# The first column pair of an up projection: norm sum, loads and sums of the second token half in another order

## The chip, the core and the metric

One core of a Trainium2 chip. Its engines work side by side, each through its own fixed list of instructions: PE (TensorE, matmuls into PSUM), DVE (VectorE), ACT (ScalarE), POOL (GpSimd) and SP, whose queue issues the DMAs of this kernel. An instruction waits on semaphores of other engines, and what is behind it on its engine waits with it. The metric is the time of one execution on the device in microseconds, as the median of several runs.

## The reference

One layer of a decoder trunk for 1024 prompt tokens and 64 sample tokens, width 1024, in float32. After the recurrent branches the layer ends with a gated convolutional feed-forward block; this is the part that matters here (the rest is left out):

```
x = x + gt1[:, None] * (merged @ p['w_out'])
h = modulate(x, p['g_norm2'], sh2, sc2)          # rmsnorm over the width, then scale and shift
up = h @ p['w_up']                               # 1024 -> 6144
uc, new_ffn_conv = causal_dwconv(ffn_conv, up, p['ffn_conv_w'], p['ffn_conv_b'])
ua, ub = jnp.split(uc, 2, axis=-1)
x = x + gt2[:, None] * ((jax.nn.gelu(ua) * ub) @ p['w_down'])
```

## The kernel before

Channels lie on the 128 partitions, tokens along the free dimension. The tokens are worked on in two halves: A (512 prompt tokens and the 64 sample tokens, 576 columns) and B (the other 512 prompt tokens). A float32 matmul is made of three passes at the rate of a rounded type: each operand is split into a rounded high part (a copy on ACT) and the remainder (a subtraction on DVE), and high x high, high x low and low x high are added up in PSUM (`split_form`, L1156, for tokens; `split_to` in `take`, L1275, for weights: `wh` and `wl` in the profile).

The up projection (`up`, L1455) goes through 24 column blocks of `w_up`, 256 columns each. Each block is a 2 x 2 block product (two column halves, even and odd width blocks, two token halves), done with seven products instead of eight. Of the weights A11, A12, A21, A22 the sums S1 to S4 are made; of the tokens the forms B11 and B21 (half A, even and odd blocks), B22 (half B, odd blocks), T1 = half B even less half A even, T2 = B22 less T1, T3 = B22 less half B even, T4 = half A odd less T2 (signs as in the code). The products are p1 = A11 B11 and p4 = A22 T4 and p6 = S2 T2 (kind "w", 576 columns), p2 = A12 B21 (also "w"), p3 = S4 B22 and p5 = S1 T1 (kind "e", 512 columns), p7 = S3 T3 (kind "p"). p1, p6, p7 and p4 add up in one PSUM tile `b`, and in between what has been reached is copied or added out of it: p4 can add into `b` only once p7's evacuation (L1400) has read it. `finish` (L1471) then does the short convolution, the gelu and the product of the two parts.

The forms are made once and kept. B11 and B21 are made early (`h2a`). The forms with half B need the second norm of half B: the output projection `w_out` (L1112) writes its result `x2d` to memory and sums its squares into `acc2`; the last two squares stay apart (`last`). `rstd_from` (L353) adds these three up over the partitions by matmuls with ones (`prs`), takes the square root on ACT and the reciprocal on DVE (`rB2`, in the profile `rstdB`). `h2b` (L1198) then reads x2d back block by block (`x2B`, three buffers), multiplies it by rB2 on DVE and applies scale and shift on ACT (`norm_raw`, L1194), subtracts half A's forms that it loads from `h2d` (`hA`), and makes B22, T1, T2, T3, T4; of the subtractions those for T3 and T4 run on POOL.

All this falls into `up_lead` (L1410), which does the first column blocks of both parts (0 and 12) together: the products p1 and p2 of both, which need only half A, then the norm sum, the conditioning row `sada` with its transposes `adap` (`ada_tail`, L1443, 16 slow float32 matmuls with `araw` from memory), `h2b`, and then the products with half B. The last p4 of each block is done within the next block.

The order in which instructions stand on each engine is fixed by a scheduler, roughly by the order of the code; `high_priority(offset=n)` lets what it encloses stand as if it had been written n steps earlier. Buffers of a pool are reused in turn, and an instruction that writes one waits for the last reader.

Of the kernel before, what the change touches and what calls it, by code (L numbers as in the profile page):

```python
# [51 lines left out]
def _body(ctx, nc, tc, a):  # L52
    V, S, G, T_ = nc.vector, nc.scalar, nc.gpsimd, nc.tensor
# [41 lines left out]
    def slot(i, name, dt=F32R):  # L95
        return pp.tile([128, 2, 576], dt, tag=f"P{i}", name=name)

    def slot512(i, name, dt=F32):
        return slot(i, name, dt).rearrange("p r x -> p (r x)")[:, :1024].rearrange("p (r x) -> p r x", r=2)
# [46 lines left out]
    def psum(tag, shape, name):  # L146
        return ps.tile(shape, F32, tag=tag, name=name, bufs={"mm": 3, "ms": 2}[tag])

    def mm(name):
        return psum("mm", [128, 2, 512], name)  # L150

    def one(tag, shape, name, dt=F32, bufs=1):
        return (rp if tag.startswith(RIGHT) else ph).tile(shape, dt, tag=tag, name=name, bufs=bufs)

    def tmp(tag, shape, name, dt=F32, bufs=2):
        return (rp if rp is not None and tag in ("xc", "h") else tp).tile(shape, dt, tag=tag, name=name, bufs=bufs)
# [196 lines left out]
    def rstd_from(acc, n, name, tag="rstd", out=None):  # L353
        pr = psum("ms", [128, 512], "prs")[:, :n]
        acc = acc if isinstance(acc, list) else [acc]
        for i, x in enumerate(acc):
            T_.matmul(pr, ones, x, start=i == 0, stop=i == len(acc) - 1)
        return rstd_of(pr, name, tag, out)

    def rstd_of(pr, name, tag="rstd", out=None):  # L360
        n = pr.shape[1]
        sd = rg("sd")[:, :n] if out is None else out[:, :n]
        S.activation(sd, pr, AF.Sqrt, scale=1.0 / D, bias=epst)
        if out is not None:
            r = out[:, :n]
        else:
            r = tmp(tag, [128, 512], name, bufs=1)[:, :n] if n > 64 else tmp("rstds", [128, 64], name, bufs=1)
        V.reciprocal(r, sd)
        return r
# [331 lines left out]
    x2d = [dp.tile([1024, 512], F32, name=f"x2d{h}") for h in range(2)]  # L701
# [445 lines left out]
    def form(n, j):  # L1147
        if n in FORMS:
            x = slot(FORMS[n][j], f"{n}_{j}")
            x = x[:, :, :512] if n == "B22" else x  # L1150
        else:
            x = one(f"{n}_{j}", [128, 2, 512], f"{n}_{j}", F32R)
        F[n, j] = x
        return x

    def split_form(x, f):  # L1156
        S.activation(x[:, 0], f, AF.Copy)  # L1157
        V.tensor_sub(x[:, 1], f, x[:, 0].bitcast(F32))  # L1158
# [8 lines left out]
    def halves(x):  # L1167
        return x.rearrange("p (h c) -> p h c", h=2)
# [25 lines left out]
    def norm_raw(dst, x, rstd, kb):  # L1194
        V.tensor_mul(x, x, rstd)
        S.activation(dst, x, AF.Identity, scale=gmod["g2"][:, kb, 0:1], bias=modT[:, 24 + kb, 0:1])

    def h2b():  # L1198

        A, ST = [], []  # L1200

        def load(tag, k, bufs):
            t = tmp(tag, [128, 632], "hA", bufs=bufs)[:, :576]
            nc.sync.dma_start(t, h2d[k])
            return t

        def nb2(dst, k):
            t = tmp("xc", [128, 632], "x2B", bufs=3)[:, :512]
            nc.sync.dma_start(t, x2d[1][k * 128:(k + 1) * 128])
            norm_raw(dst, t, rB2, k)  # L1210

        for j in range(4):
            ST.append(slot512(4 + j, f"h2B{j}"))
            nb2(ST[j][:, 1], 2 * j + 1)
            split_form(form("B22", j), ST[j][:, 1])
        for j in range(4):
            A.append(load("gl", 2 * j, 4))
        for j in range(4):
            nb2(ST[j][:, 0], 2 * j)
            V.tensor_sub(A[j][:, 32:544], ST[j][:, 0], A[j][:, 32:544])  # L1220
            split_form(form("T1", j), A[j][:, 32:544])
            G.tensor_sub(ST[j][:, 0], ST[j][:, 1], ST[j][:, 0])
        for j in range(4):
            V.tensor_sub(A[j][:, 32:544], ST[j][:, 1], A[j][:, 32:544])
            split_form(form("T2", j), A[j])
        for j in range(4):
            c = load("xc", 2 * j + 1, 3)
            G.tensor_sub(A[j], c, A[j])
        for j in range(4):
            split_form(form("T3", j), ST[j][:, 0])  # L1230
        for j in range(4):
            split_form(form("T4", j), A[j])

    def prod(acc, kind, wt, n, start=False, stop=False):
# [16 lines left out]
    class Blocks:  # L1251
# [5 lines left out]
        def load(self, *names):  # L1257
            for n in names:
                t = self.t.setdefault(n, None)
                if t is None:  # L1260
                    t = self.t[n] = wt("wr", f"w{n}", F32, WR)
                nc.sync.dma_start(t, self.w[{"A11": 0, "A12": 1, "A21": 2, "A22": 3}[n]])
# [18 lines left out]
    def wt(tag, name, dt, bufs):  # L1281
        return uw.tile([128, 512], dt, tag=tag, name=name, bufs=bufs)
# [105 lines left out]
    def evac_up(b, part, gl):  # L1388
        m0 = 24 * part + 2 * b
        raw = {}  # L1390

        def evac(i, half, y, z, e=None):
            t = tmp("rx", [128, 656], "up", bufs=4)
            o = t[:, 32:544] if half else t[:, :576]
            o = halves(o) if len(y.shape) == 3 else o
            with tc.high_priority(offset=400):
                if z is None:
                    S.activation(o, y, AF.Copy)
                elif e is not None:
                    V.tensor_sub(o, y, z)  # L1400
                    V.tensor_add(o, o, e)
                else:
                    V.tensor_add(o, y, z)  # L1403
            raw[i, half] = t
            if (i, 1 - half) in raw:
                finish(i, raw, part, m0 + i, gl, 2 * b + i)

        return evac

    def up_lead():  # L1410

        nonlocal rB2
        gl = {}
        Q = [Quad(q, evac_up(0, i, gl)) for i, q in enumerate(lead)]
        for i in range(2):
            if i == 1:
                x = slot512(2, "wx")
                Q.append(Quad(Blocks(a["w_up"][12], (("A11", x[:, 0]), ("A12", x[:, 1]))), evac_up(0, 1, gl)))
                Q[1].q.load("A11", "A12")
            Q[i].p1()  # L1420
            Q[i].p2()
        rB2 = slot(3, "rstdB2", F32)[:, 0, :512]
        rstd_from(acc2, 512, "rstdB2", out=rB2)
        e = mm("e")
        ada_tail()
        h2b()
        Q[0].p3_first(e[:, 0])
        with tc.high_priority(offset=300):
            Q[1].q.load("A21", "A22")
            Q[1].q.sums(G)  # L1430
        Q[1].p3_first(e[:, 1])
        for q in Q:
            q.p5_last()
        Q[0].p6()
        Q[0].c12()
        Q[0].p7()
        Q[0].p4()
        Q[1].p6()
        Q[1].c12()
        Q[1].p7()  # L1440
        return Q[1]

    def ada_tail():  # L1443
# [11 lines left out]
    def up():  # L1455
        pend = up_lead()
        for b in range(1, 12):
            gl = {}
            for part in range(2):
                q = Quad(blocks_of(a["w_up"][12 * part + b]), evac_up(b, part, gl))  # L1460
                q.p1()
                pend.p4()
                q.p5()
                q.p6()
                q.p2()
                q.p3()
                q.p7()
                pend = q
        pend.p4()

    def finish(i, raw, part, m, gl, k):  # L1471
        for half in range(2):
            t = fix(half, raw[i, half], m)
            n = UN[half]
            if part == 0:
                gl[i, half] = tmp("gl", [128, 632], "gl", bufs=4)
                g = gl[i, half][:, :n]
                conv_up(t, m, g)
                S.activation(g, g, AF.Gelu_apprx_tanh)
                continue  # L1480
            u, g = tmp("xc", [128, 632], "uc", bufs=3), gl[i, half]
            conv_up(t, m, u[:, :n])
            if half == 0:
                c = tmp("cs", [128, 64], "cs", bufs=2)
                G.tensor_mul(two4(s8(c)), useg(u), useg(g))
                nc.sync.dma_start(actd[0][k][:, :64], c)
            V.tensor_mul(u[:, :512], u[:, :512], g[:, :512])
            nc.sync.dma_start(actd[half][k][:, 512 * half - 512:] if half else actd[0][k][:, 64:576], u[:, :512])
# [140 lines left out]
    acc2 = w_out(0, mgA)  # L1629
# [9 lines left out]
    acc2 = w_out(1, mgB)  # L1639
# [10 lines left out]
    rB2 = None  # L1650
# [161 lines left out]
```

## Time and profile before

| | us |
|---|---|
| median of three runs | 1767.33 (1766.81 to 1769.57) |
| profiled execution, its own time | 1769.02 |
| its span, first to last instruction | 1767.2 |
| PE busy | 1707.3 (97%) |
| DVE busy | 1246.5 (71%) |
| ACT busy | 913.9 (52%) |
| POOL busy | 228.6 (13%) |

Granted TensorE clock over the span: 0.988 of full speed. The rows further down are lines of that one profiled execution. In a timeline a row begins with the start from the span's start and the duration; "x4" means four such instructions merged, and a bracket names the idle time before it and what ended it. In names, "b<-B,wh" means tile `b` written from tiles `B` and `wh`, buffer numbers left out.

### The profile page before, as it was taken

How to read it: one execution, taken by the hardware profiler on the slowest of the kernel's cores; microseconds unless marked ns; L12 is line 12 of the kernel's file. 1: busy time of each engine (PE TensorE's matmuls, PEld its weight loads, DVE VectorE, ACT ScalarE, POOL GpSimd, SP SyncE). 2: the span in 40 equal slices, each digit the busy share in tenths (PEclk: the TensorE clock that was granted, in tenths of full speed). 3: DMA queues.
4: the chain of work that ended last, by engine and by line, in shares of the span. 5: the costliest groups of instructions: out<-in, count | busy, mean ns of one | idle time of the engine just before them, and what ended most of it. 6: DMA issues, size and time to landing. Idle time of an engine off the chain costs nothing.

```text
span 1767.2 us, 29386 instructions
## 1 busy us (share of the span) xinstructions
PE 1707.3 (97%) x10542; PEld 1536.3 (87%) x10542; DVE 1246.5 (71%) x2621; ACT 913.9 (52%) x1608; POOL 228.6 (13%) x496
## 2 busy tenths in 40 slices
PE   7999999999999999999988999999999979999997
PEld 3899999899997877888766999999999968999887
DVE  8878688967846787766749877777777755336426
ACT  4557658535535588745436655555454544224224
POOL 0012110100000001020013322222222220000000
PEclk9999999999999999999998999999999989999999
DMA  8276334366646654356653222222222228546634
GB/s 302 78 231 177 99 108 132 121 192 196 204 127 203 214 177 150 118 162 189 208 173 87 74 81 84 75 74 74 74 75 79 80 85 258 166 133 188 197 96 137
DMA packets 151826, 250.87 MB, mean 142 GB/s; under 512 B 34048, under 2 KB 43264, under 8 KB 151680
## 3 DMA queue, kind: packets, MB, share of 16 engines
q1 hardware_dynamic: 151680, 248.99, 45.6%
q8 instruction: 83, 1.36, 0.3%
q14 instruction: 63, 0.52, 0.1%
HBM read 205.20 MB, written 43.73 MB: 141 GB/s over the span
## 4 chain that ended last, share of the span: by engine, by line
PE 68%; DVE 6%; DMA 4%; ACT 2%; issue 1%; SPq 0%; POOL 0%; POOLq 0%; DVEq 0%; ACTq 0%
PE mm L226 15%; PE b L1246 13%; PE mm L224 13%; PE e L1242 7%; PE mm L1533 7%; PE a L1246 4%; PE b L1249 4%; DMA al<-act 2%; DVE wlo L179 1%; DMA xB<-x 1%; PE pg L961 1%; PE pv L787 1%; PE sada L274 1%; PE sada L273 1%; PE sx L717 0%
## 5 line engine op out<-in xcount | busy, mean ns | idle before, releaser
L179 DVE TENSOR_TENSOR wlo<-raw,whi 128x512 fp32r<-128x512 f32 x310 | 214.5, 692 | 207.6 <-ACT whi L178 181.7
L178 ACT ACTIVATE whi<-raw 128x512 fp32r<-128x512 f32 x310 | 194.4, 627 | 316.2 <-PE mm L224 105.2
L224 PE MATMUL mm<-h1A,whi 128*128 128x288 f32 x1024 | 184.3, 299 | 0.0
L226 PE MATMUL mm<-h1B,whi 128*128 128x512 f32 x512 | 159.9, 393 | 0.0
L224 PEld LDWEIGHTS mm<-h1A,whi 128*128 128x128 f32 x1024 | 152.3, 190 | 0.2
L1246 PE MATMUL b<-T,wh 128*128 128x288 f32 x768 | 134.9, 297 | 2.1 <-DVE up L1403 1.3
L1246 PEld LDWEIGHTS b<-T,wh 128*128 128x128 f32 x768 | 115.1, 189 | 5.3 <-issue 1.5
L245 ACT ACTIVATE wh<-wA 128x512 fp32r<-128x512 f32 x94 | 59.2, 630 | 110.3 <-PE b L1246 42.0
L226 PEld LDWEIGHTS mm<-h1B,whi 128*128 128x128 f32 x512 | 95.6, 188 | 23.0
L224 PE MATMUL mm<-h1A,wlo 128*128 128x288 f32 x512 | 111.3, 298 | 2.1 <-DVE wlo L179 2.1
L226 PE MATMUL mm<-h1B,wlo 128*128 128x512 f32 x256 | 100.6, 393 | 0.7 <-DVE wlo L179 0.7
L224 PE MATMUL mm<-act,whi 128*128 128x288 f32 x512 | 91.8, 300 | 2.4 <-ACT act L1157 1.3
L1381 DVE SCALAR_TENSOR_TENSOR uc<-up,vec,uc 128x624 f32<-128x624 f32 (+1 forms) x96 | 76.2, 807 | 21.7 <-POOL up L1373 12.4
L1381 DVE SCALAR_TENSOR_TENSOR gl<-up,vec,gl 128x624 f32<-128x624 f32 (+1 forms) x96 | 76.2, 807 | 18.1 <-ACT gl L1379 12.6
L246 DVE TENSOR_TENSOR wl<-wA,wh 128x512 fp32r<-128x512 f32 x94 | 66.5, 708 | 26.6 <-ACT wh L245 26.1
L224 PEld LDWEIGHTS mm<-h1A,wlo 128*128 128x128 f32 x512 | 83.1, 190 | 2.3 <-DVE wlo L179 2.3
L1533 PE MATMUL mm<-act,whi 128*128 128x512 f32 (+1 forms) x304 | 82.7, 359 | 0.0
L1246 PE MATMUL b<-T,wl 128*128 128x288 f32 x384 | 82.6, 296 | 0.0
L224 PEld LDWEIGHTS mm<-act,whi 128*128 128x128 f32 x512 | 76.4, 191 | 3.9 <-DVE act L1158 2.3
L245 ACT ACTIVATE wh<-S 128x512 fp32r<-128x512 f32 x72 | 45.0, 625 | 53.8 <-PE b L1246 41.4
L224 PE MATMUL mm<-act,w 128*128 128x288 f32 x384 | 56.8, 303 | 13.3 <-ACT act L1157 11.7
L1242 PE MATMUL e<-T,wh 128*128 128x512 f32 x192 | 63.3, 409 | 5.2 <-DVE T L1158 4.2
(456 smaller groups left out, 4404.6 us busy)
## 6 DMA issues: line engine op xcount, KB each, us to landing
raw<-w_in SPq DMA_DIRECT2D x128, 256.0 KB, 2.8
raw<-w_down SPq DMA_DIRECT2D x105, 256.0 KB, 2.8
wA<-w_up SPq DMA_DIRECT2D x94, 256.0 KB, 2.7
raw<-w_ada SPq DMA_DIRECT2D x56, 256.0 KB, 3.2
act<-uc SPq DMA_DIRECT2D x48, 256.0 KB, 2.2
araw<-w_ada SPq DMA_DIRECT2D x20, 512.0 KB, 6.6
s5a<-s5d SPq DMA_DIRECT2D x16, 512.0 KB, 4.0
raw<-w_rgp SPq DMA_DIRECT2D x32, 256.0 KB, 2.8
```

The lines of the kernel that those rows point to most:

```text
L178: S.activation(hi, raw, AF.Copy)
L179: V.tensor_sub(lo, raw, hi.bitcast(F32))
L224: T_.matmul(T[m][:, h, :288], y[:, k, c], x[:, r, h * 288:(h + 1) * 288], **f)
L226: T_.matmul(T[0][:, m, tok], y[:, k, c], x[:, r, tok], **f)
L245: S.activation(hi, src, AF.Copy)
L246: V.tensor_sub(lo, src, hi.bitcast(F32))
L273: T_.matmul(sa[:18], csr[:, kb], hi, start=kb == 0, stop=False)
L1242: T_.matmul(acc, w, x, **f)
L1246: T_.matmul(acc[:, h, :288], w, x[:, h * 288:(h + 1) * 288], **f)
L1249: T_.matmul(acc[:, h, o:o + 256], w, x[:, h * 256:(h + 1) * 256], **f)
L1381: V.scalar_tensor_tensor(dst, t[:, k:k + n], fw[:, k, m:m + 1], dst, op0=OP.mult, op1=OP.add)
L1533: T_.matmul(T[:, m, tok], y[:, k, c], act[kb][:, r, tok], start=kb + n == 0, stop=kb == 23 and n == 2, skip_group_check=True)
```

## The change

In `up_lead` the products p1 and p2 of the second block are written behind the norm sum, which itself stands right behind p1 of the first block, with high priority; so do all eight loads of half B (`h2b_load`), which go straight into the slots in which the normalised half B is kept, and `norm_raw` works in place. In `h2b` all subtractions are on DVE; those for T3 stand after the T2 forms, each T4 subtraction right ahead of its form. After p5 the two blocks take turns: p6 of both, p7 of both, then the first p4 (the second stays with the next block).

```
--- before.py
+++ after.py
@@ -1195,40 +1195,42 @@
         V.tensor_mul(x, x, rstd)
         S.activation(dst, x, AF.Identity, scale=gmod["g2"][:, kb, 0:1], bias=modT[:, 24 + kb, 0:1])
 
-    def h2b():
-
-        A, ST = [], []
+    def h2b_load():
+
+        ST = [slot512(4 + j, f"h2B{j}") for j in range(4)]
+        for r in (1, 0):
+            for j in range(4):
+                k = 2 * j + r
+                nc.sync.dma_start(ST[j][:, r], x2d[1][k * 128:(k + 1) * 128])
+        return ST
+
+    def h2b(ST):
+
+        A = []
 
         def load(tag, k, bufs):
             t = tmp(tag, [128, 632], "hA", bufs=bufs)[:, :576]
             nc.sync.dma_start(t, h2d[k])
             return t
 
-        def nb2(dst, k):
-            t = tmp("xc", [128, 632], "x2B", bufs=3)[:, :512]
-            nc.sync.dma_start(t, x2d[1][k * 128:(k + 1) * 128])
-            norm_raw(dst, t, rB2, k)
-
         for j in range(4):
-            ST.append(slot512(4 + j, f"h2B{j}"))
-            nb2(ST[j][:, 1], 2 * j + 1)
+            norm_raw(ST[j][:, 1], ST[j][:, 1], rB2, 2 * j + 1)
             split_form(form("B22", j), ST[j][:, 1])
         for j in range(4):
             A.append(load("gl", 2 * j, 4))
         for j in range(4):
-            nb2(ST[j][:, 0], 2 * j)
+            norm_raw(ST[j][:, 0], ST[j][:, 0], rB2, 2 * j)
             V.tensor_sub(A[j][:, 32:544], ST[j][:, 0], A[j][:, 32:544])
             split_form(form("T1", j), A[j][:, 32:544])
-            G.tensor_sub(ST[j][:, 0], ST[j][:, 1], ST[j][:, 0])
         for j in range(4):
             V.tensor_sub(A[j][:, 32:544], ST[j][:, 1], A[j][:, 32:544])
             split_form(form("T2", j), A[j])
         for j in range(4):
-            c = load("xc", 2 * j + 1, 3)
-            G.tensor_sub(A[j], c, A[j])
-        for j in range(4):
+            V.tensor_sub(ST[j][:, 0], ST[j][:, 1], ST[j][:, 0])
             split_form(form("T3", j), ST[j][:, 0])
         for j in range(4):
+            c = load("xc", 2 * j + 1, 3)
+            V.tensor_sub(A[j], c, A[j])
             split_form(form("T4", j), A[j])
 
     def prod(acc, kind, wt, n, start=False, stop=False):
@@ -1412,18 +1414,20 @@
         nonlocal rB2
         gl = {}
         Q = [Quad(q, evac_up(0, i, gl)) for i, q in enumerate(lead)]
-        for i in range(2):
-            if i == 1:
-                x = slot512(2, "wx")
-                Q.append(Quad(Blocks(a["w_up"][12], (("A11", x[:, 0]), ("A12", x[:, 1]))), evac_up(0, 1, gl)))
-                Q[1].q.load("A11", "A12")
-            Q[i].p1()
-            Q[i].p2()
+        x = slot512(2, "wx")
+        Q.append(Quad(Blocks(a["w_up"][12], (("A11", x[:, 0]), ("A12", x[:, 1]))), evac_up(0, 1, gl)))
+        Q[1].q.load("A11", "A12")
+        Q[0].p1()
         rB2 = slot(3, "rstdB2", F32)[:, 0, :512]
-        rstd_from(acc2, 512, "rstdB2", out=rB2)
+        with tc.high_priority(offset=200):
+            rstd_from(acc2, 512, "rstdB2", out=rB2)
+            ST = h2b_load()
+        Q[0].p2()
+        Q[1].p1()
+        Q[1].p2()
         e = mm("e")
         ada_tail()
-        h2b()
+        h2b(ST)
         Q[0].p3_first(e[:, 0])
         with tc.high_priority(offset=300):
             Q[1].q.load("A21", "A22")
@@ -1431,13 +1435,12 @@
         Q[1].p3_first(e[:, 1])
         for q in Q:
             q.p5_last()
-        Q[0].p6()
-        Q[0].c12()
-        Q[0].p7()
+        for q in Q:
+            q.p6()
+            q.c12()
+        for q in Q:
+            q.p7()
         Q[0].p4()
-        Q[1].p6()
-        Q[1].c12()
-        Q[1].p7()
         return Q[1]
 
     def ada_tail():
```

On PE, around the norm sum `prs` (L357), before; `b` and `a` are the PSUM tiles of p1 and p2, of the second block here:

```order
L1246 MATMUL b<-B_3_9911,wh 128x288 x4
L1246 MATMUL b<-B_3_9911,wl 128x288 x2
L357 MATMUL prs<-acc_10135,ones 128x512
L357 MATMUL prs<-sq,ones 128x512 x2
L1246 MATMUL a<-B_0_9749,wh 128x288 x4
L1246 MATMUL a<-B_0_9749,wl 128x288 x2
```

and now, in two places; the first is within the output projection (`mm`, L226):

```order
L226 MATMUL mm<-mg_9927,whi 128x512 x2
L226 MATMUL mm<-mg_9927,wlo 128x512
L226 MATMUL mm<-mg_9934,whi 128x512
L357 MATMUL prs<-acc_10135,ones 128x512
L226 MATMUL mm<-mg_9934,whi 128x512
L226 MATMUL mm<-mg_9934,wlo 128x512
L226 MATMUL mm<-mg_9927,whi 128x512 x2
```

One pass has moved there. The second place is within p1 of the first block:

```order
L1248 MATMUL b<-B_1_9777,wh 128x288 x4
L1248 MATMUL b<-B_1_9777,wl 128x288 x2
L357 MATMUL prs<-sq,ones 128x512 x2
L1248 MATMUL b<-B_2_9850,wh 128x288 x4
L1248 MATMUL b<-B_2_9850,wl 128x288 x2
L1248 MATMUL b<-B_3_9911,wh 128x288 x4
```

The pass over `acc` is now in the last strip of the output projection, the two over `sq` are in the middle of the first product; all of the second block's products follow after them.

On SP, the DMAs issued from the end of the output projection on, before (`wx` and `wA` are blocks of `w_up`):

```order
L1262 DMA wx<-w_up 128x512 x2
L1131 DMA x2d_121<-xo 128x512 x2
L1262 DMA wA_11082<-w_up 128x512
L1448 DMA araw<-w_ada 128x2x512 x4
L1204 DMA hA<-h2d 128x576 x2
L1262 DMA wA_11084<-w_up 128x512
L1204 DMA hA<-h2d 128x576 x2
L1209 DMA x2B<-x2d_121 128x512 x8
```

and now:

```order
L1264 DMA wx<-w_up 128x512 x2
L1204 DMA h2B_10543<-x2d_121 128x512
L1204 DMA h2B_10544<-x2d_121 128x512
L1204 DMA h2B_10543<-x2d_121 128x512
L1204 DMA h2B_10544<-x2d_121 128x512
L1204 DMA h2B_10545<-x2d_121 128x512 x2
L1131 DMA x2d_121<-xo 128x512 x2
L1204 DMA h2B_10546<-x2d_121 128x512 x2
L1451 DMA araw<-w_ada 128x2x512 x4
L1213 DMA hA<-h2d 128x576 x2
L1264 DMA wA_11074<-w_up 128x512
```

The loads of x2d have moved from behind `araw` and half of `hA` to ahead of them; the last two stand behind the last two writes of x2d.

On DVE, around p7's evacuation of the first block (`up<-b`, L1400, now L1402), before; `T_` are remainders of T3 and T4 forms, `gl` convolution steps:

```order
L1158 TENSOR_TENSOR T_3_10776<-h2B_10687,T_3_10776 128x512
L1158 TENSOR_TENSOR T_0_10779<-hA,T_0_10779 128x576
L1158 TENSOR_TENSOR T_1_10782<-hA,T_1_10782 128x576
L1400 TENSOR_TENSOR up<-b,p_10807 128x512
L246 TENSOR_TENSOR wl<-wA_10809,wh 128x512
L1401 TENSOR_TENSOR up<-up,e 128x512
L1158 TENSOR_TENSOR T_2_10785<-hA,T_2_10785 128x576
L1158 TENSOR_TENSOR T_3_10788<-hA,T_3_10788 128x576
L1381 SCALAR_TENSOR_TENSOR gl<-up,vec,gl 128x624
L1381 SCALAR_TENSOR_TENSOR gl<-up,vec,gl 128x512
```

and now:

```order
L1158 TENSOR_TENSOR T_1_10768<-hA,T_1_10768 128x576
L1233 TENSOR_TENSOR hA<-hA 128x576
L1158 TENSOR_TENSOR T_2_10774<-hA,T_2_10774 128x576
L246 TENSOR_TENSOR wl<-wA_10803,wh 128x512
L1158 TENSOR_TENSOR T_3_10780<-hA,T_3_10780 128x576
L1383 SCALAR_TENSOR_TENSOR gl<-up,vec,gl 128x624
L1383 SCALAR_TENSOR_TENSOR gl<-up,vec,gl 128x512
L1383 SCALAR_TENSOR_TENSOR gl<-up,vec,gl 128x624
L1383 SCALAR_TENSOR_TENSOR gl<-up,vec,gl 128x512
L1402 TENSOR_TENSOR up<-b,p_10799 128x512
```

The evacuation stood between the second and the third remainder of T4; it now stands behind all T4 subtractions and remainders and four convolution steps.

## Rows read from the trace of the kernel before

**Rows 1.** chain of waits: start us, us, engine, tile, line, count

```profile
928.07 5.39 PE e L1242 x11
...
981.14 3.20 PE b L1246 x24
...
987.54 2.79 PE e L1242 x12
...
990.33 2.84 PE b L1249 x24
```

**Rows 2.** timeline of PE, 885 to 985: start us, us, instruction, [idle before <-releaser]

```profile
899.89 0.69 PE L1246 MATMUL b<-B,wh 128*128 128x288 f32 x4
...
909.49 1.02 PE L357 MATMUL prs<-acc,ones 128*128 128x512 f32 x2
...
912.99 0.77 PE L1246 MATMUL a<-B,wh 128*128 128x288 f32 x4 [0.77 <-DVE up L1403]
...
916.35 7.04 PE L1450 MATMUL sada<-araw,cs 128*18 128x512 f32 x16
...
971.78 0.69 PE L1246 MATMUL b<-B,wh 128*128 128x288 f32 x4
```

**Rows 3.** waits of PE, 895 to 985: us in total, times, longest

```profile
PE e L1242 <- DVE T L1158: 4.2, 3, 1.7
...
PE e L1242 <- ACT B L1157: 3.6, 1, 3.6
...
PE b L1246 <- DVE T L1158: 0.2, 1, 0.2
```

**Rows 4.** windows: stretch, length, busy us by engine, PEclk (granted clock), DMA

```profile
928.07:931.00 2.93, 2.93 (x6) 2.11 (x7) 2.60 (x5) 2.40 (x4) 0.00 (x0) 0.50 0.72 214
...
934.00:960.00 26.00, 19.36 (x75) 14.52 (x76) 25.58 (x28) 14.73 (x25) 13.03 (x8) 0.80 0.26 73
...
948.00:954.00 6.00, 5.90 (x14) 4.64 (x15) 5.72 (x7) 2.11 (x3) 3.22 (x2) 0.50 0.19 49
```

**Rows 5.** timeline of SP's queue, 885 to 985

```profile
911.25 1.97 SPq L1448 DMA_DIRECT2D araw<-w_ada  x4
...
920.54 12.38 SPq L1209 DMA_DIRECT2D x2B<-x2d  x8
```

**Rows 6.** timeline of DVE, 885 to 985

```profile
914.63 3.35 DVE L368 RECIPROCAL rstdB<-rstdB 128x512 f32<-128x512 f32 x1 [1.78 <-ACT rstdB L363]
...
938.03 1.76 DVE L1195 TENSOR_TENSOR x2B<-x2B,rstdB 128x512 f32<-128x512 f32 x1
...
943.20 0.68 DVE L1220 TENSOR_TENSOR hA<-h2B,hA 128x512 f32<-128x512 f32 x1
...
943.80 0.75 DVE L1158 TENSOR_TENSOR T<-hA,T 128x576 fp32r<-128x576 f32 x1
...
956.86 1.89 DVE L1158 TENSOR_TENSOR T<-h2B,T 128x512 fp32r<-128x512 f32 x1
...
966.75 1.52 DVE L1381 SCALAR_TENSOR_TENSOR gl<-up,vec,gl 128x624 f32<-128x624 f32 x2
```

**Rows 7.** timeline of POOL, 885 to 985

```profile
937.59 3.33 POOL L1222 TENSOR_TENSOR h2B<-h2B 128x512 f32<-128x512 f32 x2 [2.44 <-DVE hA L1220]
```

**Rows 8.** timeline of ACT, 885 to 985

```profile
900.88 1.34 ACT L1128 ACTIVATE sq<-xo 128x512 f32<-128x512 f32 x2 [3.46 <-DVE xo L1122]
...
925.97 1.52 ACT L1196 ACTIVATE h2B<-x2B,modT,gm_g 128x512 f32<-128x512 f32 x2 [1.96 <-DVE x2B L1195]
...
942.70 1.13 ACT L1157 ACTIVATE T<-h2B 128x512 fp32r<-128x512 f32 x2
```

**Rows 9.** DMA issues, 885 to 985: count, KB each, median us to landing

```profile
araw<-w_ada SPq DMA_DIRECT2D x4, 512.0 KB, 6.2
...
x2d<-xo SPq DMA_DIRECT2D x4, 256.0 KB, 2.0
```

**Rows 10.** timeline of PE at the loop's end, 1418 to 1462

```profile
1440.42 0.77 PE L1246 MATMUL b<-T,wh 128*128 128x288 f32 x4 [1.35 <-DVE up L1403]
```

## Prediction

> **What bounds the kernel now.** I read the chain of waits first. Nearly all of the run is matmuls end to end, so a change here is worth what it takes out of the pauses of PE (TensorE) in its own stretch; the chain shows the stretch of the change as the only place in the up projection where it leaves PE for long. In steady state a product costs 3.20 us ("w" kind, L1246), 2.79 ("e", L1242) or 2.84 ("p", L1249) [rows 1].
>
> The timeline of PE gives the limits of the stretch: its first product starts at 899.89, and the first product of the next column pair (`b<-B`) at 971.78 [rows 2]. That is 71.9 us. At full rate its matmuls need: four products on the first token half, 12.8; the norm sum, 2.7 (909.49 to 912.99, less a wait of 0.77); the conditioning row `sada`, 7.1, and its transposes `adap`, 0.4; four "e" products, 11.2; two p6, one p4 and two p7, 15.3. Together 49.5. So 22.4 us are pauses and slow matmuls. The view of waits names 12.9 in nine rows, from 4.2 for the T1 forms and 3.6 for the first B22 form down to 0.2 [rows 3]. The rest is half rate and restart: the first "e" product took 5.39 instead of 2.79 [rows 1], at a granted clock of 0.50, the lower level (1.2 GHz), after PE had stood nearly idle from the end of `sada` at 923.4 [rows 2]; from 948 to 954, after several short waits, it was 0.50 again [rows 4].
>
> What ends these waits last is read on SP, DVE and POOL. The eight `x2B` loads are issued from 920.54, behind `araw` (911.25) and `hA` [rows 5]; the reciprocal of the norm ends at 914.63 + 3.35 = 917.98 [rows 6]. After that DVE is late: `x2B<-x2B,rstdB` took 1.76 us at 938.03, beside two POOL subtractions (937.59, 3.33 for both [rows 7]), and an instruction of the same shape 0.68 at 943.20, with 0.60 to the start of the next [rows 6]. Eight such long ones stand between 934 and 958 (two of them in [rows 6]), as many as POOL subtractions; from 934 to 960 DVE needed 25.58 us for 28 instructions, 0.91 each [rows 4].
>
> **The change part by part.** Times are those of the profiled execution, whose 1769.02 us lie 1.7 above the median of the three runs; I take differences from it and apply them to 1767.33.
>
> *Norm sum behind half of the first product.* Three passes of 0.91 [rows 2]. One moves into the output projection, which then ends at 900.8 instead of 899.9; its sum of squares is finished where the pass now stands, within a tenth. The last two squares (900.88 to 902.2 before [rows 8]) come 0.9 later, by 903.1; half a product (1.6) runs meanwhile, and the two passes end near 904.3. From the last pass to the reciprocal it was 2.4 (912.2 to 914.63), and that takes 3.35 [rows 6]: done by 910.1, 8 earlier. The wait of 0.77 for a PSUM tile goes, since the other column's first product now stands between. PE reaches `sada` at 899.9 + 12.8 + 2.7 = 915.4 instead of 916.35.
>
> *Loads at once.* Six of the eight loads go ahead of the last two `x2d` writes; they wait for slots that the output projection's last products read (897 to 900.8). The writes wait for DVE until about 901.7 and 902.4 anyway, so this costs them nothing. The last two loads wait on SP for these writes to land, 2.0 [rows 9]: SP is held until about 904.4, and behind it `araw`, `hA` and the next weights. Four `araw` issues take 1.97 [rows 5] and land 6.2 later [rows 9], by 913; PE wants them at 915.4. Were the landings 4 us slower, PE would wait 2; before, issued at 911.25, they came in time, so I take 0.
>
> *Normalised under `sada`.* `sada` runs from 915.4 to 922.5. Ahead of the copy of its result ACT has, from about 913.4, seven scale-and-shift instructions (1.52 for two [rows 8]) and eight copies at 0.52 (1.13 for two with the tail [rows 8]): 9.5 us, to 922.9. DVE has, from 910.3, 21 instructions at 0.60 (products, remainders, subtractions, weight splits): 12.6, and up to 1.7 beside the one POOL sum that is left there, so 924.6 at most; the four B22 forms, 15 of the 21, are ready by 921. So the 3.6 for B22 goes, and the half rate behind it. What is late next is ACT: the copy of `sada`'s result, 0.6 on PE; then the last scale-and-shift, and behind it the copy `p3` out of the tile that PE writes next, 1.1; then the split of S2, which PE now wants ahead of p5, 0.45. Together 2.15. T1 is ready before p5, so the 4.2 go.
>
> *Sums on DVE.* The eight subtractions cost DVE 0.60 (512 columns) or 0.67 (576; 0.75 with the tail [rows 6]) each, 5.1 us; the eight long instructions had cost about 1.1 too much each, 8.8, which goes.
> The Trainium skill ("SBUF — State Buffer", section "Who interferes with whom") says that a DVE instruction with two SBUF inputs and a GpSimd instruction that reads SBUF keep each other out for a whole instruction. The trace agrees: 1.76 beside POOL, 0.68 alone.
>
> *Order p6, p6, p7, p7, p4.* p4 of the first column adds into the PSUM tile that p7's evacuation (L1400, now L1402) reads. On DVE that evacuation now stands behind all T4 forms and four convolution steps. PE, from 922.5: 23.7 of work (two p3, `adap`, two p5, two p6, two p7) and the 2.15, so the second p7 ends at 948.3. DVE, from 925.2 (last load multiplied, after `adap`): 45 instructions up to and with the evacuation, 29 at 0.60, 12 at 0.67, two of 624 columns at 0.78 (1.52 for two [rows 6]), two of 512 at 0.67: 28.3, so 953.5. PE waits 5.3. Where nothing stands ahead of the evacuation, at the end of the loop, the same wait was 1.35 [rows 10]: the lower bound. Above: at 0.91 each the chain ends at 966.2, a wait of 18. I take 5.3, since the POOL work behind the 0.91 is gone from this chain.
> After 5.3 us without a matmul I count one stretch at the lower clock, at the price of the earlier one, 5.39 - 2.79 = 2.6 [rows 1]; between 0 and 6.4 (p4 and the next product wholly at half rate).
> The Trainium skill ("TensorE: Matmul & The Clock Gate", Part 1, "What's actually happening") says that the clock has a half and a full state and is set by how busy PE has been, which speaks against gathering small pauses into one long one. The trace agrees on the states (0.50 and 1.00).
>
> *Sum.* The next column pair starts, in effect, at 953.6 + 3.2 + 2.6 = 959.4 instead of 971.8. Gain 12.4: 1767.33 - 12.4 = 1754.9, about 1755. Behind it, the order on every engine is that of before within two column pairs. DVE carries eight instructions of backlog (5.3 us), but the next p5 wants its weights 9.6 us after p4 begins (three products), so I give nothing back.
>
> **The rivals.**
> 1. The short waits, 2.15 between 923 and 931, already bring the lower clock. For: it was 0.50 after short waits before, too [rows 4]. Against: there T1's waits alone were 4.2 [rows 3]. Price: the second p3 and the two p5 in good part at half rate, 4 to 5: gain 8, 1759.
> 2. DVE does not get faster, because POOL was not the cause: the evacuation at 966.2, p4 12.6 later than forecast, gain 0: 1767. Against: eight long instructions to eight POOL subtractions, and 0.60 where POOL rests.
> 3. The clock holds through the long wait, or comes back at once: gain 15, 1752. For: the price rests on one fall only. Against: PE had waited less when it fell.
> 4. Slower: DVE is the bound from `sada` on, at 0.91 there too. Then the first 21 instructions take 6.5 more, the last load's multiply and with it the chain of 45 starts about 5 later and ends at 971: p4 17.5 later than forecast, 1772. It decides once the 45 take more than 0.63 + 12.4/45 = 0.91 us each. For: all sums, forms, splits and convolution steps now stand in one row on DVE. Against: as for 2.
>
> That the change doesn't do what it says has no room: loads and reciprocal stand earlier on each engine.
>
> **How the numbers follow.** Forecast (gain 10 to 14, 1753 to 1757) 0.62; rival 1, 0.18; rival 2, 0.05; rival 3, 0.10; rival 4, 0.05. A measurement of this kernel tells 0.2% (3.5 us) from no change. So faster 0.90, same 0.05 (rival 2), slower 0.05 (rival 4). The range takes in rivals 1 and 3 with what lies around them: 1750 to 1762.
>
> **What would show it.** Right: the reciprocal ends near 910 or earlier; after `sada` no wait for B22; no clock of 0.50 between 922 and 945; DVE instructions of 512 columns at 0.6 to 0.7 throughout; one PE wait of about 5 us ahead of p4, for L1402, and half rate behind it. Wrong: `sada` waiting for `araw`; a clock of 0.50 in p3 or p5; DVE instructions above 1 us with POOL idle; p4 following p7 without a pause.

## The result, and the profile after

The changed kernel takes 1758.93 us (median of 7 runs, 1754.88 to 1762.34) where the kernel before takes 1769.57 (7 runs, 1766.48 to 1772.58): 0.9939 of it, 95% interval 0.9923 to 0.9956, about 10.8 us less. Run once more in another series it was 0.9943 (0.9930 to 0.9955). The forecast was a gain of 12.4.

Times on the clock of two traces can't be set against each other directly, because the stages ahead end a few us earlier or later from run to run (the first product starts between 898.4 and 904.1 in the traces below). I therefore measure the *stretch*: from the first product of the up projection to the wait ahead of the first product of the down projection, which is the wait in these rows of TensorE's timeline (columns as in [rows 2]), of the kernel before and then of the changed one:

```profile
1455.18 5.30 PE L224 MATMUL mm<-act,w 128*128 128x288 f32 x24 [11.34 <-ACT act L1157]
```

```profile
1443.57 4.99 PE L224 MATMUL mm<-act,w 128*128 128x288 f32 x24 [11.06 <-ACT act L1157]
```

Before: 1455.18 - 11.34 - 899.89 = 543.95 us. After: 1443.57 - 11.06 - 900.50 = 532.01, 11.9 less. The second trace of the changed kernel gives 532.15; the two traces of the changed kernel agree within 0.2. One thing the stretch does not count: the pass of the norm sum over `acc` stood inside it before and stands ahead of it now (at 892.23 below), and the three passes took 2.7 [rows 2]. So about 0.9 of the 11.9 is moved and not saved, and about 11.0 is left, which agrees with the 10.1 to 10.8 by timing. All of the 11.9 is there when the second column pair starts: TensorE's timeline of the changed kernel, to be read against [rows 2]:

```profile
892.23 1.13 PE L357 MATMUL prs<-acc,ones 128*128 128x512 f32 x2
...
900.50 0.69 PE L1248 MATMUL b<-B,wh 128*128 128x288 f32 x4
...
902.17 1.98 PE L357 MATMUL prs<-sq,ones 128*128 128x512 f32 x4
...
915.28 7.04 PE L1453 MATMUL sada<-araw,cs 128*18 128x512 f32 x16
...
949.39 0.40 PE L1251 MATMUL b<-T,wl 128*128 128x256 f32 x2
955.89 1.30 PE L1248 MATMUL b<-T,wh 128*128 128x288 f32 x4 [6.10 <-ACT gl L1482]
...
957.47 1.16 PE L1248 MATMUL b<-T,wh 128*128 128x288 f32 x4
...
958.84 0.70 PE L1248 MATMUL b<-T,wh 128*128 128x288 f32 x4
...
960.44 0.69 PE L1248 MATMUL b<-B,wh 128*128 128x288 f32 x4
```

From the first product to the next pair's it was 71.9 us and is 59.9. Groups of four matmuls at the start of p4 take 1.30 and 1.16 where a later one takes 0.70: half rate. The view of waits, 890 to 985, where [rows 3] had nine rows:

```profile
PE b L1248 <- ACT gl L1482: 6.1, 1, 6.1
PE adap L328 <- ACT adat L1455: 1.4, 1, 1.4
PE e L1244 <- ACT p L1304: 1.0, 1, 1.0
PE b L1248 <- ACT wh L245: 0.5, 1, 0.5
```

The waits for B22 and T1 are gone, and one long wait ahead of p4 has come. The windows (columns as in [rows 4]) show the clock at 1.00 through p3, p5, p6 and p7; its only fall comes within that wait and lasts into p4:

```profile
922.00:938.00 16.00, 13.15 (x57) 9.70 (x57) 15.52 (x28) 10.86 (x20) 0.00 (x0) 1.00 0.21 68
938.00:949.80 11.80, 11.79 (x94) 11.54 (x92) 11.52 (x19) 7.19 (x12) 1.09 (x2) 1.00 0.21 53
949.80:955.90 6.10, 0.01 (x1) 0.04 (x1) 6.10 (x10) 5.45 (x8) 0.00 (x0) 0.67 0.21 78
955.90:962.00 6.10, 6.10 (x36) 6.10 (x37) 6.08 (x10) 1.17 (x2) 2.10 (x3) 0.77 0.01 1
```

DVE's timeline has the reciprocal and the two ends of the chain ahead of p4, the last multiplication by it and the evacuation of p7:

```profile
904.91 3.35 DVE L368 RECIPROCAL rstdB<-rstdB 128x512 f32<-128x512 f32 x1 [2.80 <-ACT rstdB L363]
...
925.41 0.68 DVE L1195 TENSOR_TENSOR h2B<-h2B,rstdB 128x512 f32<-128x512 f32 x1
...
952.18 2.96 DVE L1383 SCALAR_TENSOR_TENSOR gl<-up,vec,gl 128x624 f32<-128x624 f32 x4
955.06 1.28 DVE L1402 TENSOR_TENSOR up<-b,p 128x512 f32<-128x512 f32 x2
```

The loads are issued from 897.29 and `araw` at 906.28 on SP's queue, instead of 920.54 and 911.25 [rows 5]:

```profile
897.29 3.52 SPq L1204 DMA_DIRECT2D h2B<-x2d  x6
...
906.28 1.92 SPq L1451 DMA_DIRECT2D araw<-w_ada  x4
```

### The profile page after: what moved, and what is told of

Read it like the earlier page. It is cut to its first block, busy times and chain, and to the rows that moved or that the text cites. A ratio compares the mean times of both kernels' runs of the same rounds, so it can differ in the third digit from the quotient of the medians.

```text
span 1754.7 us, 29379 instructions
## 1 busy us (share of the span) xinstructions
PE 1698.0 (97%) x10542; PEld 1531.1 (87%) x10542; DVE 1241.7 (71%) x2629; ACT 913.7 (52%) x1608; POOL 219.6 (13%) x488
## 4 chain that ended last, share of the span: by engine, by line
PE 69%; DVE 5%; DMA 4%; ACT 2%; issue 1%; POOL 0%; SPq 0%; POOLq 0%; DVEq 0%; ACTq 0%
PE mm L226 16%; PE b L1248 13%; PE mm L224 12%; PE e L1244 7%; PE mm L1536 7%; PE a L1248 4%; PE b L1251 3%; DMA al<-act 2%; DMA xB<-x 1%; PE pv L787 1%; PE pg L961 1%; DVE wlo L179 1%; PE sada L274 1%; PE sada L273 1%; DMA tgb<-tg 0%
## 5 line engine op out<-in xcount | busy, mean ns | idle before, releaser
L226 PE MATMUL mm<-h1B,whi 128*128 128x512 f32 x512 | 159.9, 393 | 0.0
L226 PEld LDWEIGHTS mm<-h1B,whi 128*128 128x128 f32 x512 | 95.6, 188 | 23.1
L226 PE MATMUL mm<-h1B,wlo 128*128 128x512 f32 x256 | 100.7, 393 | 0.7 <-DVE wlo L179 0.7
L1383 DVE SCALAR_TENSOR_TENSOR uc<-up,vec,uc 128x624 f32<-128x624 f32 (+1 forms) x96 | 76.0, 806 | 22.2 <-POOL up L1375 12.4
L1248 PE MATMUL b<-B,wh 128*128 128x288 f32 x384 | 67.2, 296 | 0.0
```

The costliest lines, as they stand in the source:

```text
L226: T_.matmul(T[0][:, m, tok], y[:, k, c], x[:, r, tok], **f)
L1248: T_.matmul(acc[:, h, :288], w, x[:, h * 288:(h + 1) * 288], **f)
L1383: V.scalar_tensor_tensor(dst, t[:, k:k + n], fw[:, k, m:m + 1], dst, op0=OP.mult, op1=OP.add)
```

## The experiments

Each kernel was timed beside the kernel before: e1 to e4, e5 to e8 and e9 to e11 are one series each. "Stretch" is as above, one trace each, against 543.95. In every kernel but e7 the pass over `acc` has left the stretch, so about 0.9 of its "less than before" is not saved; differences among these kernels are not touched by that.

| kernel | parts of the change in it | stretch | less than before | ratio, 95% interval |
|---|---|---|---|---|
| e5_norm_early | norm | 542.06 | 1.9 | 0.9994 [0.9986, 1.0003] |
| e7_subs_dve | subtractions | 541.19 | 2.8 | 0.9986 [0.9977, 0.9995] |
| e6_early | norm, loads | 534.86 | 9.1 | 0.9951 [0.9938, 0.9964] |
| e3_subs_pool | norm, loads, order | 532.69 | 11.3 | 0.9942 [0.9928, 0.9957] |
| changed kernel | all | 532.01 | 11.9 | 0.9939 [0.9923, 0.9956] |
| e11_after | all, again | 532.15 | 11.8 | 0.9943 [0.9930, 0.9955] |
| e2_fill | all, wait filled | 532.96 | 11.0 | 0.9931 [0.9919, 0.9943] |
| e1_inplace | all, evacuation freed | 530.23 | 13.7 | 0.9916 [0.9902, 0.9929] |
| e9_order_adap | e4, `adap` later | 528.93 | 15.0 | 0.9925 [0.9912, 0.9939] |
| e4_old_order | norm, loads, subtractions | 528.74 | 15.2 | 0.9913 [0.9900, 0.9927] |
| e10_order_sums | e9, weight sums later | 528.48 | 15.5 | 0.9927 [0.9910, 0.9944] |
| e8_better | all, freed, `adap` and sums later | 526.57 | 17.4 | 0.9898 [0.9886, 0.9911] |

**e5: the norm alone.** Of the change, only the norm sum moves behind half of the first product.

> The kernel before with the first part of the change alone: the norm sum behind half of the first product; loads, places of the sums and order of products as before. Theory (norm and loads must both come earlier): the reciprocal ends 7 to 8 us earlier, near 910, but the x2B loads are still issued at 920 behind araw and hA, so TensorE still waits about 3.6 us for B22 and falls to half rate; sada starts 1 us earlier; 0 to 2 us less than before. Rival (the late norm alone held B22): the 3.6 and the 2.6 go, 6 to 7 us less.

The interval includes no change: the theory held. The reciprocal starts at 907.06 and ends at 910.4, but the loads still stand on SP's queue behind `araw`, `hA` and two weight blocks, the last of which goes out at 918.97, and TensorE still waits for B22 (a row of SP, of DVE and of the waits):

```profile
919.35 14.11 SPq L1209 DMA_DIRECT2D x2B<-x2d  x8
```

```profile
907.06 3.35 DVE L368 RECIPROCAL rstdB<-rstdB 128x512 f32<-128x512 f32 x1 [2.81 <-ACT rstdB L363]
```

```profile
PE e L1242 <- ACT B L1157: 3.2, 1, 3.2
```

**e6: norm and loads.** The eight subtractions and the order of products are those of before.

> The changed kernel without its last two parts: norm sum early and loads at once, normalised in place, but the eight subtractions on POOL at their places of before and the products in the order of before. Theory: the wait for B22 (3.6) and the half rate behind it (2.6) go, the waits for T1 stay in part because eight instructions of DVE are still long beside POOL (1.7 to 1.8); 6 to 8 us less than before, next pair at 964 to 966. Rival (these loads only shift the wait to the T forms, all of which hang on DVE): under 3 us less, next pair past 969.

9.1 in the stretch, 8.2 without the moved pass, so at the upper end of what was expected; the next pair starts 62.7 after the first product. B22 and T1 have left the view of waits. What stands there now is put down to ACT:

```profile
PE b L1249 <- ACT wh L245: 4.1, 2, 3.6
PE e L1245 <- ACT p L1305: 3.3, 1, 3.3
```

**e7: the subtractions alone.** `G.tensor_sub` becomes `V.tensor_sub` at both places in `h2b` of the kernel before.

> The kernel before with one part alone: the eight subtractions for T3 and T4 on DVE. Theory (shared port): no DVE instruction of 512 columns over 0.9 us in the stretch, DVE's work from 934 to 958 about 3.7 us shorter; the waits for T1 and for the copies behind shrink by 2 to 4 us; 2 to 4 us less than before. Rival (DVE gets 5.1 us more to do and nothing back): the T forms come later, 3 to 5 us more than before.

2.8 less, and the ratio's interval lies below 1: the theory held. DVE's groups of 930 to 960 have no long instruction left (mean ns behind the busy time), where [rows 6] has 1.76:

```profile
L1195 DVE TENSOR_TENSOR x2B<-x2B,rstdB 128x512 f32<-128x512 f32 x5 | 3.4, 685 | 0.1
L1158 DVE TENSOR_TENSOR T<-hA,T 128x512 fp32r<-128x512 f32 x4 | 2.7, 686 | 0.0
```

**e3: the subtractions back on POOL.** The reverse test, in the changed kernel:

```diff
-            V.tensor_sub(ST[j][:, 0], ST[j][:, 1], ST[j][:, 0])
+            G.tensor_sub(ST[j][:, 0], ST[j][:, 1], ST[j][:, 0])
...
-            V.tensor_sub(A[j], c, A[j])
+            G.tensor_sub(A[j], c, A[j])
```

> The changed kernel with the eight subtractions for T3 and T4 on POOL again. Theory (shared port): DVE is rid of eight instructions (5.1 us), but about eight others beside them take 1.7 to 1.8 us instead of 0.68 (8.8 us); the first evacuation of p7 ends about 3.7 us later than 955.7 and the next pair starts near 964; 3 to 4 us more than the changed kernel. Rival (POOL does not slow DVE): the chain on DVE is 5.1 us shorter, p4 starts near 951, the next pair near 955; 5 us less.

The mechanism held, its price did not. DVE's long instructions are back, and one POOL row shows the subtractions beside them:

```profile
922.61 3.01 DVE L1223 TENSOR_TENSOR hA<-h2B,hA 128x512 f32<-128x512 f32 x3
...
935.76 3.76 DVE L1226 TENSOR_TENSOR hA<-h2B,hA 128x512 f32<-128x512 f32 x2
...
941.39 4.36 DVE L1158 TENSOR_TENSOR T<-h2B,T 128x512 fp32r<-128x512 f32 x3
...
957.79 0.68 DVE L1402 TENSOR_TENSOR up<-b,p 128x512 f32<-128x512 f32 x1
```

```profile
935.25 3.72 POOL L1233 TENSOR_TENSOR hA<-hA 128x576 f32<-128x576 f32 x2 [1.90 <-DVE T L1158]
```

(The DVE rows down to 941.39 hold five long ones; with the rows at 925.54 and 932.12 there are eight, each about 1.1 longer.) The evacuation ends 56.8 after the first product instead of 55.2, so 1.6 later and not 3.7. TensorE now pauses in several shorter waits, and the clock does not fall ahead of p4; it fell in the first p3 instead (0.58 from 926 to 930), behind a wait of 1.65 for `adat`. Net 0.7, which the timing can't tell from nothing. The Trainium skill ("SBUF — State Buffer", "Who interferes with whom") says that a DVE instruction with two SBUF inputs contends with a GpSimd instruction that reads SBUF; e3 and e7 agree on it from both sides, with 1.76 and 1.89 beside a POOL subtraction [rows 6] and 0.69 without one (e7). They show the times, not the port.

**e1: the evacuation freed.** What holds p4? The view of waits names the gelu on ACT. In the program p4 waits for the subtraction L1402 on DVE, which writes a fifth `up` tile where there are four, and so stands behind the convolution steps that read the first; these wait for a tile of T4's. The edit takes the `up` tile out of it:

```diff
-                    V.tensor_sub(o, y, z)
-                    V.tensor_add(o, o, e)
+                    V.tensor_sub(z, y, z)
+                    V.tensor_add(o, z, e)
```

> The changed kernel with one edit: the evacuation of p7 subtracts into the SBUF tile p3 itself and adds e into the up tile afterwards, so that the PSUM tile of p4 comes free without a new up tile. Theory (DVE's queue and the fourth up tile held the evacuation): both subtractions come right behind their p7, p4 starts within 1 us of the end of the second p7 (949.8 in the changed kernel), is then paced by the T4 forms, and the next column pair starts at 954 to 956 instead of 960.4; 4 to 6 us less than the changed kernel. Rival (the gelu on ACT, L1482, which the view of waits names as the releaser, is what p4 waits for): p4 not before 955.8, no gain.

p4 starts without a wait, 49.1 after the first product instead of 55.4, though the gelu comes only at 954.7: the theory held and the named releaser was the wrong one (the traces of e2 and e3 name `DVE up L1402`). But only 1.8 of the 7.4 us (6.10 of wait and 1.35 of half rate) stay in the stretch, where 4 to 6 were expected; the timing gives 4 to 5, with an interval that overlaps the changed kernel's. TensorE now runs both p4 in one row (947.53 to 954.36) and then waits again, and runs at half rate longer than before:

```profile
947.53 0.70 PE L1248 MATMUL b<-T,wh 128*128 128x288 f32 x4
...
956.89 1.33 PE L1248 MATMUL b<-B,wh 128*128 128x288 f32 x4 [2.53 <-DVE up L1403]
...
958.50 1.16 PE L1248 MATMUL b<-B,wh 128*128 128x288 f32 x4
```

```profile
945.54 0.68 DVE L1402 TENSOR_TENSOR p<-b,p 128x512 f32<-128x512 f32 x1
...
948.09 0.69 DVE L1402 TENSOR_TENSOR p<-b,p 128x512 f32<-128x512 f32 x1
...
956.16 0.68 DVE L1403 TENSOR_TENSOR up<-p,e 128x512 f32<-128x512 f32 x1
```

The next p1 takes the PSUM tile `e`, which the second addition L1403 still reads; that one does need the `up` tile. From this p1 to the next `a` product it took 12.06 for 9.19 of work at full rate (3.20 + 2.79 + 3.20): 2.9 lost to the clock, 2.5 to the wait, 5.4 of the 7.4 given back.

**e2: the wait filled.** 22 matmuls, whose sum nothing reads, between p7 and p4.

```diff
+        fl = psum("ms", [128, 512], "fill")
+        for k in range(22):
+            T_.matmul(fl, F["T4", 0][:, 0, :128], F["T4", 0][:, 0, :512], start=k == 0, stop=k == 21)
         Q[0].p4()
```

> The changed kernel with 22 extra matmuls of 512 columns (5.1 us, their sum is never read) on TensorE between the last p7 and p4, inside the wait of 6.1 us. Theory (the slow start of p4 is the lower clock after the wait): the wait's end stays at 955.9, p4 then takes 3.2 us instead of 4.55 at a granted clock of 1.00, the next pair starts 1.35 us earlier, at 959.1; in total time under 0.1%, not to be told from no change. Rival (p4 is slow because its T4 forms or its weights come late): p4 still takes 4.5 us.

p4 takes 961.55 - 958.25 = 3.30 instead of 4.55: its slow start was the clock, and cost 1.25. The time is the same as the changed kernel's within its interval. In this trace the clock fell elsewhere, in the first p3, and p4 started 1.35 later after the first product (56.74 to 55.39):

```profile
925.85 0.42 PE L328 MATMUL adap<-vec,adat 18*128 18x18 f32 x4 [1.38 <-ACT adat L1458]
...
927.19 1.06 PE L1244 MATMUL e<-B,wh 128*128 128x512 f32 x2
...
958.25 0.80 PE L1248 MATMUL b<-T,wh 128*128 128x288 f32 x4 [1.00 <-DVE up L1402]
```

**e4: the order of before.** The changed kernel with p6, p7, p4 of the first column ahead of the second's.

```diff
-        for q in Q:
-            q.p6()
-            q.c12()
-        for q in Q:
-            q.p7()
-        Q[0].p4()
+        Q[0].p6()
+        Q[0].c12()
+        Q[0].p7()
+        Q[0].p4()
+        Q[1].p6()
+        Q[1].c12()
+        Q[1].p7()
```

> The changed kernel with the products in the order of before (p6, p7, p4 of the first column, then p6, p7 of the second). Theory (the order only chooses where TensorE waits for the T4 forms, whose last is ready near 952.3 on DVE whatever the order): the wait moves in front of or into the first p4, 4 to 7 us in all, and the next pair starts between 958 and 963; within 0.2% of the changed kernel. Rival (the new order itself bought the wait of 6.1 us and the lower clock): without it no wait above 2 us, next pair at 953 to 955, 5 to 7 us less.

My theory fell; the rival was nearer. The stretch is 3.3 shorter, no wait is above 1.4, and the clock is 1.00 throughout:

```profile
PE adap L328 <- ACT adat L1456: 1.4, 1, 1.4
PE b L1248 <- ACT up L1400: 1.0, 1, 1.0
PE b L1248 <- ACT wh L245: 1.0, 2, 0.5
PE b L1248 <- ACT t L1304: 1.0, 1, 1.0
PE e L1244 <- ACT p L1304: 1.0, 1, 1.0
```

```profile
946.17 0.69 DVE L1402 TENSOR_TENSOR up<-b,p 128x512 f32<-128x512 f32 x1
```

Here the evacuation of the first p7 comes fourth in the row of `up` tiles and goes through at 946.17, and TensorE does p4 piece by piece, as T4 forms come, between pieces of the second column's p6 and p7: the work that the new order had put ahead of the wait now lies in it. The waits named come to 5.8, against 9.0 and the 1.35 of half rate; 1.2 of this difference I can't place.

**e9, e10, e11: on from e4, and the changed kernel beside them.** e9 puts the transposes of the conditioning row behind p5; e10 also puts the four weight sums of the next pair's first block behind the T4 forms.

```diff
-        ada_tail()
+        adat = ada_tail()
...
             q.p5_last()
+        ada_fin(44, 4, adat)
```

> e4_old_order (the changed kernel with the products in the order of before) with one more edit: the transposes of the conditioning row stand behind the p5 products. Theory: the wait of 1.4 us for adat goes and nothing takes its place but ACT's copy of p3, which comes up to 1.1 us earlier against TensorE; 0.5 to 1.4 us less than e4_old_order, about 1751.5. Rival (the wait for ACT only moves to the copy of p3, as in e8_better, where it was 2.1): no gain over e4_old_order.

> e9_order_adap with the weight sums of the next column pair (four instructions of DVE) at a lower priority, behind the T4 forms. Theory (T4 forms still pace the end of the stretch): the last T4 form is ready 2.4 us earlier and the second column's products no longer mix with p4; 1 to 3 us less than e9_order_adap, about 1749.5. Rival (with the old order the T4 forms are no longer waited for; e4_old_order showed no wait for one): same as e9_order_adap within 0.1%, or up to 2 us more from weight splits that come late in the next pair.

> The changed kernel itself once more, unedited, on the chip of the two kernels above. Theory (its order of products costs what e4_old_order saved): 10 to 12 us less than before and 3 to 5 us more than e9_order_adap on the same chip; again a wait of about 6 us ahead of p4 and the clock at 0.50 behind it. Rival (the difference to e4_old_order came from another chip or run): within 1.5 us of e9_order_adap.

e9's rival held: no gain over e4, and most of the wait for `adat` (1.4) moves to ACT's copy of p3 (1.0 to 2.1). Not all of it: e9's clock also fell at the start of the next pair (0.50 from 958 to 960), behind a wait of 1.8 where e4's was 1.0, and e4's clock did not fall. e10 wins nothing on e9 either; there the clock fell behind the copy of p3 (0.50 from 932 to 934). Two rows of e9:

```profile
PE e L1244 <- ACT p L1304: 2.1, 1, 2.1
```

```profile
956.23 0.80 PE L1248 MATMUL b<-B,wh 128*128 128x288 f32 x4 [1.77 <-ACT up L1400]
```

e11 repeats the changed kernel's waits (`6.1` ahead of p4 again) and is 3.5 us slower than e9 by the medians of the same series (1756.85, 1753.31), 3.2 by the stretch. So the order's cost is no matter of chips.

**e8: a version that beats both.** The freed evacuation of e1, `adap` later, and the weight sums later (priority 100 instead of 300 for the first block of the next pair).

> Made to beat the changed kernel: p7's subtraction into p3 as in e1_inplace; the weight sums of the next column pair (four instructions of DVE, 2.4 us, at 937 to 944) at a lower priority, behind the T4 forms; and the transposes of the conditioning row, which nothing in this stretch needs, behind the p5 products (their wait of 1.4 us goes). Theory (DVE's queue to the last T4 form sets the stretch): p4 follows p7 with under 1 us of wait at the full clock and the next pair starts at 950 to 953 instead of 960.4; 7 to 10 us less than the changed kernel, near 1749. Rival (what DVE puts off comes back in the next pair): TensorE waits there for S1 or for evacuations, and no more is left than what e1_inplace gains.

1751.08 us beside 1767.53, ratio 0.9898 [0.9886, 0.9911], below the changed kernel's interval; with e4's it overlaps. The stretch is 5.4 shorter than the changed kernel's, less than the 7 to 10 hoped for (the timing gives 7 to 8). With the sums out of the way DVE's additions come in time, and the next pair gives back 1.0 (`up`, below) where it was 5.4 in e1; both p4 follow p7 without a wait and run at full rate, from 953.72 to 960.12. The clock fell once, behind the first of these waits (0.50 from 932 to 935). What is left:

```profile
PE e L1244 <- ACT p L1305: 2.1, 1, 2.1
PE a L1248 <- ACT up L1401: 1.0, 1, 1.0
PE b L1248 <- ACT wh L245: 0.4, 1, 0.4
```

## Why the prediction was right

The measured gain is 10.1 to 10.8 us by timing and 11.0 in the traces (11.9 in the stretch less the moved pass); the sum said 12.4 and had counted that pass. The mechanism is the one it named. Its steps, with times after the first product, which the forecast put at 900.8 and the trace has at 900.50:

- *Norm and loads.* Reciprocal done at 7.8 (forecast: by 9.3), `sada` reached at 14.8 (14.6) without a wait for `araw`, B22 not waited for: right. e5 and e6 show that the early norm needs the early loads: 0.6 thousandths alone, 4.9 together. Whether the loads alone would do was not run.
- *Short waits.* Forecast 0.6 + 1.1 + 0.45; measured 1.39 + 0.97 + 0.49. `adat` came late because ACT copied three T forms first (its row starts at 922.66 and takes 1.66; `adat` follows at 924.22). Another 1.0 until the end of p7 stands in no wait that the view names. Forecast for the end of p7: 47.5; measured 49.3.
- *DVE's chain.* Forecast to run from 24.4 to 52.7, with 5.3 of wait; it ran from 24.9 to 55.2, with a wait of 6.10. It held 46 instructions, one more than I had counted, and three idle gaps of 0.2; at 30.3 us, 0.66 each. Rivals 2 and 4 (0.91 each) are out.
- *Half rate.* The forecast's 2.6 was mis-sized: 1.35 in the trace and 1.25 in e2. I had taken it from an "e" product that ran wholly at the lower clock [rows 1]; there TensorE was at work again about 1 us after the fall (0.50 in the windows from 927 on, the product from 928.07). Here the granted clock was 0.50 from 952 on, so that nearly 4 us of the slow time lay inside the wait, and it was back within 3 us of the start of p4 (955.89; full rate by 958.84). Rival 3 (no fall) is out. Rival 1 (a fall after the short waits) did not happen in this trace; it did in e2 (1.6) and in e3.
- p4 started 2.6 later than forecast (55.4 to 52.8) and was slowed 1.25 less, so half of one error hid behind the other: the next pair started at 59.9, forecast 58.6. Part of the hit is luck.

What the prediction passed over: it charged 5.3 + 2.6 to the new order of products without asking what the old order would cost on top of the other three parts. It would have cost less: the change gives away 3.3 us by it, of the 15.2 in e4's stretch (3.5 by timing between e9 and e11). The clue stood in the working: the evacuation "stands behind all T4 forms and four convolution steps" because it asks for a fifth `up` tile where four are had; in the old order it takes the fourth, and only p4's own evacuation asks for the fifth. e1 shows that the `up` tile is what held p4; a pool of five, which would test the buffer by itself, was not run.

And the price of a part depends on what is late beside it. The eight subtractions on DVE are worth 2.8 alone (e7), 6.1 on top of norm and loads with the old order (e4 against e6), and 0.7 with the new one (the changed kernel against e3), where L1402 ends the last wait ahead of p4 in both. These are differences of single traces, and the clock has a part in them: it fell twice in e6 (0.57 from 934 to 938, 0.69 from 952 to 956) and never in e4, and once each in e3 and the changed kernel.

## What to carry to other kernels

When a change has several parts, price each against the others in place, not against the kernel before: a part can lose what another one gained, and the total still looks good. Before work of another column is moved ahead of a late product, count the buffers that its results hold until then; when the evacuation behind it must wait for one of them, either free it of that buffer and take other work out of its way (e8, 5.4 less in the stretch), or keep the order that mixes small pieces of both columns (e4, 3.3 less). And a wait that is removed is worth only what the next tile's release, some products later, lets through: 1.8 of 7.4 in e1.

## What the runs showed of the hardware

The fall of the clock was not decided by the length of the pause alone. After the same wait for `adat` (1.38 to 1.39) at the same place it stayed at 1.00 in the changed kernel (both traces), e1 and e4, and was 0.56 and 0.58 in the two windows behind it in e2; after one of 1.65 it fell in e3 and not in e6, and after a wait of 2.1 for the copy of p3 it fell in e8 and e10 and not in e9. One fall cost 1.25 us at p4 of the changed kernel, about 1.6 in e2, e8 and e10, 2.6 in the kernel before and 2.9 in e1. The Trainium skill ("TensorE: Matmul & The Clock Gate", Part 1, "What's actually happening") puts it down to how busy TensorE has been; these traces show the two states that it names, but not from which pause on it falls.
